# A channel mixer's first products in seven block products for eight, in a two-layer hybrid trunk

## The chip, the cores and the metric

One core of a Trainium2 chip runs the whole program. The metric is the device time of one execution in microseconds (us). TensorE multiplies matrices; VectorE (DVE in the rows), ScalarE (ACT) and GpSimd (POOL) work element by element; SyncE (SP) issues the loads. All data sits in an on-chip memory (SBUF); matmuls write into PSUM banks, which VectorE and ScalarE read.

## The reference

Two layers follow each other. Each has an attention part (three token mixers and projections), which the change leaves as it is, and then a channel mixer, cut here to what matters:

```python
def conv_glu(h, w1, conv_w, conv_b, w2):
    a, u = jnp.split(h @ w1, 2, axis=-1)
    a = dwconv_centred(a, conv_w) + conv_b
    return (jax.nn.silu(a) * u) @ w2
...
hl = modulate(xl, norm2_g[l], mod_l[3], mod_l[4])
xl = xl + mod_l[5] * conv_glu(hl, ffn_w1[l], ffn_conv_w[l], ffn_conv_b[l], ffn_w2[l])
```

`h` has 1024 features, `w1` maps them to 2 x 2816 columns, `w2` maps 2816 back to 1024. `modulate` is a root-mean-square norm with a scale and a shift per feature. The convolution runs over three neighbouring tokens. Layer 0 works on 512 latent and 256 context tokens (768), layer 1, the last, on the 512 latent ones alone.

## The kernel before, in words

Activations lie with features on the 128 partitions and tokens along the columns, so `h` is eight tiles of 128 features. Each float32 value is split into a rounded high half and a low half (the rest), and a product is three passes: high by high, low weight by high, high weight by low. A weight unit (`wunit`) loads up to 1024 columns as a raw tile (`wr`, two buffers), ACT writes the high half and VectorE or, for every third unit, GpSimd the low half into a tile `wl` (four buffers), and then the raw buffer is free. SP's queue holds the loads in program order, so a load that waits for a buffer holds back those behind it.

In the channel mixer (`mixer` in `layer`), w_1 is taken in 22 pairs of 128-column chunks, an a-chunk f and a u-chunk 22 + f. For each, 8 feature tiles x 3 passes = 24 matmuls of 512 columns, in layer 0 also 24 of 256, add up in a PSUM bank `pf`. `use_a` then makes the convolution and the first half of silu from the bank, `use_u` multiplies by u, `then` splits the result into `g`, high and low. After a group of five or six pairs (`FGROUPS`) `down` multiplies the group by w_2 into eight chunks of the result, each added to `x` by `residual`.

The order on each engine is fixed when the program is built: a planner (`sch`) holds jobs in program order, takes the matmuls of the current and the next one, and inserts the deferred work of other engines by estimated times. The norm ahead of the mixer (`norm_chain`) writes `hh` and `hl`; it starts when the sums of squares of the tokens are there, for layer 1 in two halves of 256 tokens, because there the last three chunks of w_o, the product before it, run in halves (`sg`).

Tile names in the rows: `wr`, `wl` weights raw and split; `x` the residual stream, `xn`, `hh`, `hl` the norm's results; `ff`, `g` the gated product; `th`, `acc` scratch; `pf`, `pm`, `pb` PSUM banks. All instructions go through one wrapper, so their line is L167 throughout; the raw loads have L500.

Of the kernel before, what the change touches and what calls it, by code (L numbers as in the profile page):

```python
# [34 lines left out]
FGROUPS = ((0, 6), (6, 6), (12, 5), (17, 5))  # L35
# [139 lines left out]
class Sched:  # L175
# [124 lines left out]

    def met(self, need):
        return need() if callable(need) else self.room(need)

    def piece(self):
# [35 lines left out]
        if self.cur is not None and self.nxt is None:  # L340
            n = len(self.jobs[0][1]) if self.jobs and self.jobs[0][0]() else 2
            if self.cur[0] + n + (self.parked[0][0] if self.parked else 0) <= NWL and (n <= 2 or self.left["w"] > NSLOT):
                self.nxt = self.pick()
# [35 lines left out]
def trunk(  # L379
# [19 lines left out]
    wl_ = ctx.enter_context(tc.tile_pool(name="wl", bufs=NWL))  # L399
# [93 lines left out]
    def wunit(src, n):  # L493

        while sch.left["r"] < 1:
            sch.flush([g for g in sch.groups if g[4]][:1])
        sch.left["r"] -= 1
        hl = wl_.tile([P, 2, 1024], F32R, tag="wl", name="wl")
        raw = wr_.tile([P, 1024], F32, tag="wr", name="wr")
        nc.sync.dma_start(out=raw[:, 0:n], in_=src)  # L500
        lo_n[0] += 1
        eng = "G" if lo_n[0] % lo_n[1] == 0 else "V"

        def halves():
# [1230 lines left out]
    for l in range(DEPTH):  # L1735
# [172 lines left out]
        hh, hl = h_tiles(nt)  # L1908
        ready = {"n": HALF if last else LAT}

        def fin(a, b, cond):
            sch.spawn(norm_chain(cond, stats, x, hh, hl, am, m48, 24, a, b, 0 if a < LAT else 1, ready), -1)
# [4 lines left out]
        sch.jobs.append((always, *fprojs(specs[-3:], mh, ml, nt, None, sg)))  # L1917
# [7 lines left out]

        def mixer():
            for f0, nf in FGROUPS:
                gh, gl_ = [], []
                for f in range(f0, f0 + nf):
                    ff = []  # L1930

                    def use_a(a, b, v, ps, f=f, ff=ff):
                        if not ff:
                            ff.extend(slot(2, nt, "ff"))
                        yield from conv(ff[0][:, a:b], ps, cf[:, f, :], bf[:, f:f + 1])
                        yield from silu2(ff[0][:, a:b], ff[1][:, a:b])
                        ff.append(a)

                    def use_u(a, b, v, ps, ff=ff):
                        yield lambda: a in ff[2:]  # L1940
                        yield "V"
                        V.tensor_tensor(out=ff[0][:, a:b], in0=ff[0][:, a:b], in1=ps, op=ALU.mult)

                    def then(ff=ff, gh=gh, gl_=gl_):
                        hi, lo = slot(2, nt, "g", F32R)
                        split(hi, lo, ff[0], G)
                        gh.append(hi)
                        gl_.append(lo)
                    specs = [(w_1[l, f], use_a, None), (w_1[l, FC + f], use_u, then)]
                    for e in [specs] if f == 0 else [specs[:1], specs[1:]]:  # L1950
                        yield fprojs(e, hh, hl, nt, KB, None, ready if f == 0 else None)
                end = f0 == FGROUPS[-1][0]

                def down(us, cs, gh=gh, gl_=gl_, nf=nf, end=end):
                    yield lambda: len(gl_) == nf
                    units = [(cols(u, 0), residual(x, gate2, c, post if end else None), None) for u, c in zip(us, cs)]
                    yield from mm3s(units, gh, gl_, nt, nf, None, True, sg if len(cs) > 1 else None)

                for cs in [(c,) for c in range(KC - 3)] + [(5, 6, 7)] if end else [(c,) for c in range(KC)]:
                    yield [(w_2[l, c, :, f0 * P:(f0 + nf) * P], nf * P) for c in cs], lambda us, cs=cs, down=down: down(us, cs)  # L1960
# [130 lines left out]
```

## Time and profile before

| | |
|---|---|
| median of 3 runs | 2910.19 us (2909.45 to 2910.57) |
| profiled execution | 2909.93 us |
| its span (first to last instruction) | 2908.2 us |
| granted TensorE clock, mean | 0.994 of full speed |
| TensorE busy | 2835.2 us, 97% |
| VectorE / ScalarE / GpSimd busy | 1699.2 / 1226.8 / 811.3 us |

The span is what the trace covers; the profiled time is 1.7 us longer. Busy shares are means over stages that differ: the mixer of layer 0 lies at about 1109 to 1662 us, that of layer 1 at about 2541 to 2905 us.

### The profile page before, as it was taken

Reading aid. Unit: us, or ns where it says so; the run is one execution under the profiler, and the core shown is the slowest. Engines: PE = TensorE matmul, PEld = TensorE weight load, DVE = VectorE, ACT = ScalarE, POOL = GpSimd, SP = SyncE. Lnnn points to the kernel's source line nnn. Section 1 sums busy time; section 2 is a strip of 40 time slices with the busy share of each in tenths; the row PEclk is TensorE's granted clock in tenths of the full one; section 3 lists DMA queues with packets and bytes.
Section 4 is the critical chain, followed back from the end, with each engine's and each line's share of the span. In section 5 each row is a group of like instructions: output and inputs, shape, how many; then the busy total and the mean of one; then the engine's idle time right before and its main releaser. Section 6 shows DMA issues by size and latency. Waiting matters only on the chain.

```text
span 2908.2 us, 48877 instructions
## 1 busy us (share of the span) xinstructions
PE 2835.2 (97%) x19304; PEld 2460.5 (85%) x19304; DVE 1699.2 (58%) x3433; ACT 1226.8 (42%) x2522; POOL 811.3 (28%) x832
## 2 busy tenths in 40 slices
PE   7999999999999999999999999999999999999999
PEld 5888898888788888888888889898878788888888
DVE  4555767868766545333334456577787866553343
ACT  4444556645443224222222345466654443343332
POOL 3414231123322432112112242441123333422221
PEclk9999999999999999999999999999999999999999
DMA  8242211241312631121212321212131316323332
GB/s 312 90 147 77 68 49 55 62 157 59 113 57 97 221 109 59 51 73 53 72 58 68 97 75 55 61 59 62 57 122 44 132 66 203 127 85 107 97 98 87
DMA packets 100117, 271.99 MB, mean 94 GB/s; under 512 B 14209, under 2 KB 26417, under 8 KB 99889
## 3 DMA queue, kind: packets, MB, share of 16 engines
q1 hardware_dynamic: 88800, 247.31, 26.5%
q10 hardware_dynamic: 10800, 20.98, 1.8%
q8 instruction: 152, 2.49, 0.4%
q0 software_dynamic: 288, 0.59, 0.1%
q14 instruction: 77, 0.62, 0.1%
HBM read 240.56 MB, written 28.86 MB: 93 GB/s over the span
## 4 chain that ended last, share of the span: by engine, by line
PE 56%; DVE 3%; POOL 2%; issue 1%; ACT 1%; DMA 1%; SPq 0%; POOLq 0%; ACTq 0%; DVEq 0%
PE pf L167 46%; PE pm L167 7%; PE pb L167 2%; DVE wl L167 0%; POOL wl L167 0%; POOL m L167 0%; POOL pres L167 0%; DVE mx L167 0%; DMA th<-gd 0%; DVE dnw L167 0%; DVE oacc L167 0%; DVE pres L167 0%; POOL rn L167 0%; POOL rtmp L167 0%; DVE p L167 0%
## 5 line engine op out<-in xcount | busy, mean ns | idle before, releaser
L167 PE MATMUL pf<-hh,wl 128*128 128x512 f32 (+1 forms) x4192 | 1022.6, 359 | 9.9 <-ACT hh L167 6.2
L167 PEld LDWEIGHTS pf<-hh,wl 128*128 128x128 f32 x4192 | 698.1, 190 | 105.0 <-ACT hh L167 9.2
L167 POOL TENSOR_TENSOR wl<-wr,wl 128x512 fp32r<-128x512 f32 (+3 forms) x258 | 326.0, 1280 | 940.0 <-ACT wl L167 934.1
L167 PE MATMUL pf<-hl,wl 128*128 128x512 f32 (+1 forms) x2096 | 575.7, 359 | 0.9 <-POOL hl L167 0.6
L167 ACT CAST wl<-wr 128x512 fp32r<-128x512 f32 (+3 forms) x620 | 341.2, 588 | 491.0 <-PE pf L167 423.4
L167 PEld LDWEIGHTS pf<-hl,wl 128*128 128x128 f32 x2096 | 361.0, 190 | 47.6 <-POOL hl L167 1.8
L167 PE MATMUL pf<-wl,hh 128*128 128x256 f32 (+2 forms) x1664 | 321.7, 288 | 0.0
L167 PE MATMUL pf<-g,wl 128*128 128x512 f32 (+1 forms) x1629 | 307.3, 350 | 0.0
L167 PEld LDWEIGHTS pf<-g,wl 128*128 128x128 f32 x1629 | 263.8, 189 | 42.3 <-ACT g L167 1.9
L167 DVE TENSOR_TENSOR wl<-wr,wl 128x512 fp32r<-128x512 f32 (+4 forms) x362 | 263.3, 751 | 51.5 <-ACT wl L167 49.7
L167 PEld LDWEIGHTS pf<-wl,hh 128*128 128x128 f32 x1664 | 264.5, 192 | 5.9 <-issue 4.1
L167 PE MATMUL pf<-wl,hl 128*128 128x256 f32 (+2 forms) x832 | 241.1, 290 | 0.0
L167 DVE SCALAR_TENSOR_TENSOR x<-pf,gate,x 128x512 f32<-128x512 f32 (+1 forms) x126 | 80.4, 640 | 243.6 <-PE pf L167 237.0
L167 PE MATMUL pm<-dnw,pres 128*128 128x128 f16 (+1 forms) x1824 | 195.3, 236 | 6.2 <-POOL pres L167 3.0
L167 DVE SCALAR_TENSOR_TENSOR ff<-pf,cf,ff 128x511 f32<-128x511 f32 (+1 forms) x132 | 86.9, 658 | 184.5 <-ACT ff L167 183.2
L167 ACT ACTIVATE p<-pb,nb,r 128x768 f32<-128x768 f32 (+1 forms) x160 | 145.1, 908 | 104.5 <-DVE nb L167 82.7
L167 PE MATMUL pf<-ohl,wl 128*128 128x512 f32 (+1 forms) x864 | 171.6, 359 | 1.5 <-DVE ohl L167 0.7
L167 PEld LDWEIGHTS pf<-ohl,wl 128*128 128x128 f32 x864 | 143.9, 191 | 26.4 <-DVE ohl L167 1.8
L167 PEld LDWEIGHTS pf<-wl,hl 128*128 128x128 f32 x832 | 160.1, 192 | 2.7 <-issue 2.5
L167 DVE TENSOR_REDUCE mx<-pb 128x1 f32<-128x768 f32 (+1 forms) x160 | 133.5, 845 | 41.1 <-PE pb L167 39.9
L167 ACT CAST dnw<-pm 128x512 f16<-128x512 f32 x144 | 83.9, 585 | 143.8 <-PE pm L167 140.3
L167 PEld LDWEIGHTS <-pres 128*128 128x128 f16 (+1 forms) x1440 | 87.3, 98 | 58.2 <-issue 32.3
(246 smaller groups left out, 4083.9 us busy)
## 6 DMA issues: line engine op xcount, KB each, us to landing
wm<-in_w_mod_dram SPq DMA_DIRECT2D x96, 512.0 KB, 5.4
wr<-in_w_dram SPq DMA_DIRECT2D x88, 512.0 KB, 3.6
wr<-in_w_f_dram SPq DMA_DIRECT2D x80, 512.0 KB, 3.6
wr<-in_w_t_dram SPq DMA_DIRECT2D x32, 512.0 KB, 3.7
wr<-in_w_br_dram SPq DMA_DIRECT2D x24, 512.0 KB, 3.6
wr<-in_w_dram SPq DMA_DIRECT2D x32, 384.0 KB, 3.1
wr<-in_w_dram SPq DMA_DIRECT2D x32, 320.0 KB, 2.9
gd<-th ACTq DMA_DIRECT2D x24, 384.0 KB, 2.3
```

What stands on the lines that cost most here:

```text
L167: ins = f(*args, **kw)
```

## The change

The first products of a pair of chunks are regarded as a 2 x 2 block product. The features are halved (four tiles of 128 each), the weights of a pair are the blocks a1, a2 (the a-chunk by upper and lower features) and u1, u2, and the tokens are halved too. With seven products of sums of blocks in place of eight products of blocks, the four result blocks come out as sums. Per pair that is 7 x 4 x 3 = 84 matmuls of half the tokens (384 columns in layer 0, 256 in layer 1), where there were 48 of 512 and, in layer 0, 48 of 256.

The sums have to be made. For the weights `block_weights` loads both raw tiles and holds them until four sums and seven splits into halves are done; for the activations `Blocks.fill` makes, after the norm, seven sets of four tiles (B11, B21, B22 and T1 to T4), split again. `block_products` runs the seven products into three banks and takes them out in seven evictions; `block_gated` makes convolution and gate from SBUF, with edges of one column where the halves of tokens meet. The tile `wl` of 2 x 1024 becomes two tiles of 1024, in all eight buffers. Groups are smaller in layer 0, one pair is run ahead of each group's w_2 products, and the w_2 units of layer 0 take two chunks each. w_o's last three chunks are no longer in halves in layer 1.

```diff
-FGROUPS = ((0, 6), (6, 6), (12, 5), (17, 5))
+FGROUPS = ((3, 3, 3, 3, 3, 3, 4), (6, 6, 5, 5))
...
-    wl_ = ctx.enter_context(tc.tile_pool(name="wl", bufs=NWL))
+    wl_ = ctx.enter_context(tc.tile_pool(name="wl", bufs=2 * NWL))
...
+            for k in range(KH):
+                plain("B22", k, KH + k, 1)
+
+                V.scalar_tensor_tensor(out=t(KH + k, 1), in0=t(KH + k, 1), scalar=self.dsh[:, k, v:v + 1], in1=t(k, 1), op0=ALU.add, op1=ALU.subtract)
+                G.tensor_tensor(out=t(k, 1), in0=t(k, 1), in1=t(k, 0), op=ALU.subtract)
+                V.scalar_tensor_tensor(out=t(k, 0), in0=t(KH + k, 1), scalar=sh(k), in1=t(k, 0), op0=ALU.add, op1=ALU.add)
+                summed("T2", k, k, 0, V)
+                yield 0
...
+    def block_weights(l, f, ops):
+
+        raws = []
+        for j in (f, FC + f):
+            yield lambda: sch.left["r"] > 0
+            sch.left["r"] -= 1
+            raw = wr_.tile([P, 1024], F32, tag="wr", name="wr")
+            nc.sync.dma_start(out=raw, in_=w_1[l, j])
+            raws.append(raw)
+        (a1, a2), (u1, u2) = [(r[:, 0:512], r[:, 512:1024]) for r in raws]
+
+        def operand(src, eng):
+            yield lambda: sch.ring() > 0
+            sch.held += 1
+            o = wl_.tile([P, 1024], F32R, tag="wl", name="wl")
+            yield "S"
+            S.copy(out=o[:, 0:512], in_=src)
+            yield eng
+            (G if eng == "G" else V).tensor_tensor(out=o[:, 512:1024], in0=src, in1=f32(o[:, 0:512]), op=ALU.subtract)
+            ops.append(o)
+
+        def add(out, p, q, op):
+            yield "G"
+            G.tensor_tensor(out=out, in0=p, in1=q, op=op)
+        yield from operand(a1, "V")
+        yield from operand(a2, "V")
+        yield from add(a1, a1, u1, ALU.subtract)
+        s2 = th_.tile([P, TOK], F32, tag="th", name="th")[:, 0:512]
+        yield from add(s2, u2, a1, ALU.subtract)
+        yield from operand(s2, "V")
+        yield from add(u1, u1, u2, ALU.add)
+        yield from operand(u1, "V")
+        yield from operand(a1, "G")
+        yield from add(a2, a2, s2, ALU.subtract)
+        yield from operand(a2, "V")
+        sch.left["r"] += 1
+        yield from operand(u2, "G")
+        sch.left["r"] += 1
...
+        for j, (nm, bk) in enumerate(zip(PROD, "ABADBDB")):
...
+            for i, (e, d) in enumerate(((0, 0), (1, 0), (0, 1))):
+                for k in range(KH):
...
+                    T.matmul(p, lhsT=ops[j][:, e * 512 + k * P:e * 512 + (k + 1) * P], rhs=bl.at(nm, k, d, c0, c1),
+                             start=(j < 5 and i == 0 and k == 0), stop=(i == 2 and k == KH - 1), skip_group_check=True)
...
+        yield "G"
+        G.tensor_tensor(out=y, in0=y, in1=u, op=ALU.mult)
+        yield "V"
+        V.scalar_tensor_tensor(out=y, in0=th, scalar=1.0, in1=y, op0=ALU.add, op1=ALU.mult)
+        yield "S"
+        S.copy(out=hi, in_=y)
+        yield "G"
+        G.tensor_tensor(out=lo, in0=y, in1=f32(hi), op=ALU.subtract)
...
-        sch.jobs.append((always, *fprojs(specs[-3:], mh, ml, nt, None, sg)))
+        sch.jobs.append((always, *fprojs(specs[-3:], mh, ml, nt)))
```

GpSimd's order in layer 1, inside a run of pairs. Before, its rows are low halves of every third weight unit and g's low half:

```order
722 L167 TENSOR_TENSOR wl<-wr,wl 128x512 [waits PE_49,DMAHW1_49,Activation_49,Pool_49]
723 L167 TENSOR_TENSOR wl<-wr,wl 128x512 [waits Activation_49]
724 L167 TENSOR_TENSOR g<-ff,g 128x512 [waits Activation_49]
725 L167 TENSOR_TENSOR wl<-wr,wl 128x512 [waits DMAHW4_49,Activation_49,Pool_49]
726 L167 TENSOR_TENSOR wl<-wr,wl 128x512 [waits Activation_49]
727 L167 TENSOR_TENSOR g<-ff,g 128x512 [waits Activation_49] x2
```

These rows span three pairs or so. Of the change, one pair (`wr<-wr` and `th<-wr` are sums of weights, `th<-th,au` is y times u):

```order
861 L167 TENSOR_TENSOR wr<-wr 128x512 [waits DMAHW1_49,DMAHW2_49,DVE_49,Pool_49]
862 L167 TENSOR_TENSOR th<-wr 128x512 [waits Pool_49]
863 L167 TENSOR_TENSOR wr<-wr 128x512
864 L167 TENSOR_TENSOR wr<-wr,th 128x512 [waits DVE_49,Pool_49]
865 L167 TENSOR_TENSOR wl<-wr,wl 128x512 [waits Activation_49]
866 L167 TENSOR_TENSOR wl<-wr,wl 128x512 [waits PE_49,Activation_49]
867 L167 TENSOR_TENSOR th<-th,au 128x512 [waits Activation_49]
868 L167 TENSOR_TENSOR g<-th,g 128x512 [waits Activation_49]
```

Eight instructions stand for one pair, the first of which waits for both loads, and the low halves come after all four sums; in other pairs y times u stands between the two low halves.

SP's order at the w_1 loads of layer 1, first before, where each load waits for one engine, GpSimd for every third:

```order
611 L500 DMA wr<-in_w_dram 128x1024 [waits DMAHW7_49,Pool_49]
612 L500 DMA wr<-in_w_dram 128x1024 [waits DMAHW0_49,DVE_49]
613 L500 DMA wr<-in_w_dram 128x1024 [waits DMAHW1_49,DVE_49]
614 L500 DMA wr<-in_w_dram 128x1024 [waits DMAHW2_49,Pool_49]
615 L500 DMA wr<-in_w_dram 128x1024 [waits DMAHW3_49,DVE_49]
```

And of the change, three pairs:

```order
622 L1842 DMA wr<-in_w_dram 128x1024 [waits DMAHW1_49,DVE_49,Pool_49]
623 L1842 DMA wr<-in_w_dram 128x1024 [waits DMAHW2_49,Pool_49]
624 L1842 DMA wr<-in_w_dram 128x1024 [waits DMAHW3_49,DVE_49,Pool_49]
625 L1842 DMA wr<-in_w_dram 128x1024 [waits DMAHW4_49,Pool_49]
626 L1842 DMA wr<-in_w_dram 128x1024 [waits DMAHW6_49,DVE_49,Pool_49]
627 L1842 DMA wr<-in_w_dram 128x1024 [waits DMAHW5_49,DVE_49]
```

Each pair's loads now wait for VectorE and GpSimd work on the pair before, in the two buffers.

VectorE's order in layer 1 at the norm before the mixer. Before, scalings (`xn<-pm,am,x`) and low halves (`hl`) of the first 256 tokens alternate, with weights and residuals between:

```order
2889 L167 SCALAR_TENSOR_TENSOR xn<-pm,am,x 128x256
2890 L167 SCALAR_TENSOR_TENSOR hl<-xn,modF,hh 128x256 [waits Activation_49]
2891 L167 SCALAR_TENSOR_TENSOR xn<-pm,am,x 128x256 x3
2892 L167 TENSOR_TENSOR wl<-wr,wl 128x512 [waits DMAHW0_49,PE_49]
2893 L167 SCALAR_TENSOR_TENSOR hl<-xn,modF,hh 128x256 [waits Activation_49]
```

Of the change, a part of the longer row of sums that follows the scalings (`xn<-xn` are sums, `bt` the home of T1, T2 and T4):

```order
3129 L167 SCALAR_TENSOR_TENSOR xn<-xn,dsh 128x256 [waits DVE_49] x2
3130 L167 SCALAR_TENSOR_TENSOR hh<-xn,modF,hh 128x256 [waits Activation_49]
3131 L167 SCALAR_TENSOR_TENSOR xn<-xn,modF 128x256 [waits Pool_49] x2
3132 L167 SCALAR_TENSOR_TENSOR xn<-xn,dsh 128x256 [waits DVE_49]
3133 L167 TENSOR_TENSOR bt<-xn,bt 128x256 [waits Activation_49]
```

The sums of one tile pass from VectorE to GpSimd and back before the block's halves can be made.

## Rows read from the trace of the kernel before

**Rows 1.** The page's head and busy time by engine

```profile
span 2908.2 us, 48877 instructions
...
PE 2835.2 (97%) x19304; PEld 2460.5 (85%) x19304; DVE 1699.2 (58%) x3433; ACT 1226.8 (42%) x2522; POOL 811.3 (28%) x832
```

**Rows 2.** The chain that ended last (start us, us, what)

```profile
1128.12 533.81 PE pf L167 x3065
...
2547.11 357.76 PE pf L167 x1646
```

**Rows 3.** Windows in both mixers (us, busy by engine, clock, DMA share, GB/s)

```profile
1200.00:1275.00 75.00, 75.00 (x433) 66.27 (x432) 25.34 (x43) 15.93 (x30) 10.75 (x9) 1.00 0.24 69
...
2700.00:2775.00 75.00, 75.00 (x331) 61.86 (x330) 30.14 (x46) 24.28 (x44) 15.53 (x14) 1.00 0.33 100
```

**Rows 4.** TensorE's timeline (start us, us, engine, line, operation, count)

```profile
1820.78 0.40 PE L167 MATMUL pf<-wl,hh 128*128 128x256 f32 x2
...
1827.62 0.40 PE L167 MATMUL pf<-wl,hh 128*128 128x256 f32 x2
...
2555.72 0.62 PE L167 MATMUL pf<-hl,wl 128*128 128x512 f32 x2
...
2574.77 0.62 PE L167 MATMUL pf<-hl,wl 128*128 128x512 f32 x2
```

**Rows 5.** A raw load in the chain, and DMA issues (size, us to landing)

```profile
1106.22 4.01 DMA wr<-in_w_dram
...
1110.31 0.62 ACT wl L167
...
wm<-in_w_mod_dram SPq DMA_DIRECT2D x96, 512.0 KB, 5.4
wr<-in_w_dram SPq DMA_DIRECT2D x88, 512.0 KB, 3.6
```

**Rows 6.** GpSimd's and VectorE's timelines where they meet

```profile
1166.10 1.84 POOL L167 TENSOR_TENSOR g<-ff,g 128x768 fp32r<-128x768 f32 x1 [13.08 <-ACT g L167]
1166.57 1.92 DVE L167 TENSOR_TENSOR wl<-wr,wl 128x512 fp32r<-128x512 f32 x1 [0.56 <-ACT wl L167]
...
2502.87 2.55 POOL L167 TENSOR_TENSOR wl<-wr,wl 128x512 fp32r<-128x512 f32 x2 [4.16 <-ACT wl L167]
2503.53 0.75 DVE L167 SCALAR_TENSOR_TENSOR x<-pf,gate,x 128x512 f32<-128x512 f32 x1 [0.61 <-PE pf L167]
...
2567.50 1.29 DVE L167 TENSOR_TENSOR wl<-wr,wl 128x512 fp32r<-128x512 f32 x2
```

**Rows 7.** GpSimd's groups by shape in layer 0's mixer (busy, mean ns)

```profile
L167 POOL TENSOR_TENSOR g<-ff,g 128x768 fp32r<-128x768 f32 x22 | 40.6, 1844 | 156.0 <-ACT g L167 156.0
...
L167 POOL TENSOR_TENSOR hl<-xn,hh 128x256 fp32r<-128x256 f32 x4 | 3.0, 740 | 9.5 <-ACT xn L167 9.5
```

**Rows 8.** Timelines at layer 0's norm: VectorE, then TensorE behind pair 0

```profile
1098.05 0.75 DVE L167 SCALAR_TENSOR_TENSOR x<-pf,gate,x 128x512 f32<-128x512 f32 x1 [4.69 <-PE pf L167]
...
1103.95 0.75 DVE L167 SCALAR_TENSOR_TENSOR xn<-pm,am,x 128x512 f32<-128x512 f32 x1 [0.76 <-PE pm L167]
...
1107.98 2.05 DVE L167 SCALAR_TENSOR_TENSOR xn<-pm,am,x 128x512 f32<-128x512 f32 x3
...
1123.98 0.87 DVE L167 SCALAR_TENSOR_TENSOR hl<-xn,modF,hh 128x256 fp32r<-128x256 f32 x2
...
1131.10 1.09 PE L167 MATMUL pf<-hh,wl 128*128 128x512 f32 x4
```

**Rows 9.** TensorE's timeline at layer 1's norm

```profile
2531.93 6.48 PE L167 MATMUL pf<-mhl,wl 128*128 128x256 f32 x52
2541.47 0.71 PE L167 MATMUL pf<-hh,wl 128*128 128x256 f32 x4 [3.06 <-DVE x L167]
...
2554.79 1.09 PE L167 MATMUL pf<-hh,wl 128*128 128x512 f32 x4
```

**Rows 10.** Windows with the granted clock (the column after POOL)

```profile
1731.00:1737.00 6.00, 5.54 (x30) 5.55 (x31) 0.98 (x1) 2.16 (x4) 0.70 (x1) 0.50 0.32 87
...
2538.40:2541.50 3.10, 0.04 (x2) 0.06 (x1) 3.10 (x4) 0.21 (x2) 2.25 (x2) 1.00 0.14 40
```

More of the change, by code (lines that the diff above doesn't have):

```diff
@@ L299, in take_up, with ring @@
         return [len(units), body([u for u, _ in units]), must, [g for _, g in units]]
+    def ring(self):
+        return 2 * (NWL - sum(j[0] for j in (self.cur, self.nxt, self.parked and self.parked[0]) if j)) - self.held
     def met(self, need):
@@ L341, in piece @@
             n = len(self.jobs[0][1]) if self.jobs and self.jobs[0][0]() else 2
-            if self.cur[0] + n + (self.parked[0][0] if self.parked else 0) <= NWL and (n <= 2 or self.left["w"] > NSLOT):
+            if (2 * n <= self.ring() and (n <= 2 or self.left["w"] > NSLOT)
+                    and (n == 0 or not self.held or self.left["r"] > 0 or any(g[4] for g in self.groups))):
                 self.nxt = self.pick()
@@ L497, in wunit @@
         sch.left["r"] -= 1
-        hl = wl_.tile([P, 2, 1024], F32R, tag="wl", name="wl")
+        hl = [wl_.tile([P, 1024], F32R, tag="wl", name="wl") for _ in range(2)]
         raw = wr_.tile([P, 1024], F32, tag="wr", name="wr")
-        nc.sync.dma_start(out=raw[:, 0:n], in_=src)
+        srcs = src if isinstance(src, list) else [src]
+        w = n // len(srcs)
+        for i, s in enumerate(srcs):
+            nc.sync.dma_start(out=raw[:, i * w:(i + 1) * w], in_=s)
         lo_n[0] += 1
@@ L1720, in trunk, with block_view @@
+    def block_view(t, H, a, b):
+        if H == LAT // 2:
+            return t[:, a:b]
+        c0, c1 = (0, LAT // 2) if a == 0 else (LAT // 2, H)
+        return t.rearrange("p (h c) -> p h c", h=2)[:, :, c0:c1]
     x = chunks8(TOK, "x")
@@ L1907, in trunk @@
         am = norm_gain(l, 1, m48)
[L1908 to L1909 removed]
+        bl = Blocks(nt)
         def fin(a, b, cond):
[L1912 removed]
+            sch.spawn(bl.chain(cond, stats, x, am, m48, a, b, 0 if a < LAT else 1), -1)
         add, stats = norm_acc(x, nt, None, fin, th_.tile([P, TOK], F32, tag="th", name="th"))
@@ L1924, in trunk @@
         V.tensor_scalar(out=gate2, in0=m48[:, 40:48, :], scalar1=0.5, scalar2=None, op0=ALU.mult)
-        def mixer():
[L1927 to L1960, printed above, removed]
@@ new lines, in trunk, with pair, body, run @@
+        gs = []
+        def pair(f):
+            def body(us):
+                ops, au = [], []
+                sch.defer(block_weights(l, f, ops))
+                def run():
+                    au.extend(slot(2, nt, "au"))
+                    if f == 0:
+                        cuts = [(0, LAT // 2)] + ([(LAT // 2, bl.H)] if bl.H > LAT // 2 else [])
+                    else:
+                        cuts = [(0, bl.H)]
+                    for c0, c1 in cuts:
+                        yield from block_products(bl, ops, au, c0, c1, f == 0, c1 == bl.H)
+                    sch.defer(block_gated(bl, au, cf, bf, f, gs))
+                return run()
+            return [], body
@@ new lines, in down, with body @@
+        def down(f0, nf, cs, end):
+            packed = len(cs) > 1 and not end
+            srcs = [w_2[l, c, :, f0 * P:(f0 + nf) * P] for c in cs]
+            def body(us):
+                yield lambda: len(gs) >= f0 + nf
+                uses = [residual(x, gate2, c, post if end else None) for c in cs]
+                order = [(s, i) for s in sg or segs(nt) for i in range(len(cs))] if len(cs) > 1 and end else [(s, i) for i in range(len(cs)) for s in segs(nt)]
+                for (a, b, v), i in order:
+                    ps = bank()
+                    w = cols(us[0], i * nf * P) if packed else cols(us[i], 0)
+                    for n, (e, d) in enumerate(((0, 0), (1, 0), (0, 1))):
+                        for k in range(nf):
+                            T.matmul(ps[:, 0:b - a], lhsT=w(k)[e], rhs=block_view(gs[f0 + k][d], bl.H, a, b),
+                                     start=(n == 0 and k == 0), stop=(n == 2 and k == nf - 1))
+                            yield
+                    sch.defer(uses[i](a, b, v, ps[:, 0:b - a]), ps)
+            return [(srcs, len(cs) * nf * P)] if packed else [(s, nf * P) for s in srcs], body
@@ new lines, in mixer @@
+        def mixer():
+            ahead, f0 = 0, 0
+            for nf in FGROUPS[l]:
+                end = f0 + nf == FC
+                while ahead < min(FC, f0 + nf + 1):
+                    yield pair(ahead)
+                    ahead += 1
+                if end:
+                    css = [(c,) for c in range(KC - 3)] + [(5, 6, 7)]
+                else:
+                    n = 2 if 2 * nf * P <= 1024 else 1
+                    css = [tuple(range(c, c + n)) for c in range(0, KC, n)]
+                for cs in css:
+                    yield down(f0, nf, cs, end)
+                f0 += nf
```

146 lines of the change are left out of this document (140 added, 6 removed).

## The prediction

> **What bounds the kernel now.** I read the page's head first: TensorE is busy for 97% of a span of 2908.2 us, VectorE for 58%, GpSimd for 28% [rows 1]. Then the chain of work that ended last: both channel mixers lie on it as one unbroken piece each, nothing but the matmuls into `pf`, 533.8 us in layer 0 and 357.8 us in layer 1 [rows 2]. The windows inside the mixers say the same: 75.00 us of TensorE in 75 us, GpSimd at 11 to 16 us and VectorE near 30 [rows 3]. So a matmul taken out of a mixer is worth its full pace, as long as the other engines keep up. The question is whether they still do, because the change pays for the saved products with additions on GpSimd and VectorE and with two raw weight buffers that are held longer.
>
> The profiled execution took 2909.93 us, 1.7 us more than its span and 0.26 us under the median of 2910.19. All sums are made against it; the forecast in median terms is 0.3 us higher, which is nothing here.
>
> **The change, part by part.**
>
> *Saved matmul time.* At a steady place 84 matmuls of 512 columns start within 2555.72 and 2574.77, 226.8 ns each; 57 of 256 columns start within 1820.78 and 1827.62, 120.0 ns each [rows 4]. No 384-column one is in the trace; scaling the one pace gives 170, the other 180, and the middle, (226.8 + 120.0)/2 = 173.4 ns, I take. Layer 0, per pair of chunks: before 48 x (226.8 + 120.0) = 16.65 us, after 7 x 12 = 84 x 173.4 = 14.57 us, 2.08 saved. Layer 1: before 48 x 226.8 = 10.89, after 84 x 120.0 = 10.08, 0.81 saved. For 21 pairs in each layer (pair 0 is counted below): 43.7 + 17.0 = **60.7 us saved**, between 49 and 67 by the two ends of the 384-column price. The Trainium skill (TensorE: Matmul & The Clock Gate, Back-to-back issue gap) gives N/2.4 + 2.5 ns for a matmul of N columns. As an estimate from that page, 2.0 and 1.2 us would be saved per pair, 66 in all; the rows' own paces lie 11 ns above it at either size, and I keep the rows.
>
> *GpSimd and VectorE do not run beside each other on data in SBUF.* At 1166.10 GpSimd starts a subtraction of 1.84 us; VectorE starts its own at 1166.57 and needs 1.92 us, ending 0.55 us after GpSimd's, where two such in a row take 1.29 us, 0.65 each. But a VectorE instruction with one operand in PSUM takes 0.75 us in the middle of two GpSimd ones [rows 6]. So a VectorE instruction with two SBUF operands waits until GpSimd's has ended. The Trainium skill says so in kind (GPSIMD Engine Reference, Specifications: the SBUF interfaces are shared with VectorE, with contention where a VectorE instruction has two SBUF inputs), without a price; the trace agrees, and shows the price to be the rest of the running GpSimd instruction.
>
> *Layer 1, a steady pair.* New on GpSimd are four 512-column sums and two low halves, beside y·u and g's low half: eight instructions of 1.28 us (2.55 for two [rows 6]), 10.2 us. VectorE has five low halves of weights, two convolution taps and the tanh gate with two SBUF operands: 8 x 0.65 = 5.2 us. Since the two exclude each other, 15.4 us of work stand against 10.08 us of TensorE. The evictions have an operand in PSUM and are not in this sum. The order inside a pair gives the same figure. From both raw tiles in: ACT's high half of a1 0.62 [rows 5], low halves of a1 and a2 2 x 0.65 (1.9); three sums 3.84 (5.8); s2's low half (6.4), the fourth sum (7.7), u1+u2's low half (8.4), GpSimd's low half of a1-u1 (9.6), a2-s2's low half (10.3), GpSimd's of u2 (11.5). Only now is the second of the only two raw buffers free; the next load took 4.01 us to be readable [rows 5]: 15.5. y·u, the gate and the convolution fit into that load's time. I take **15.5 us per pair**. Without the exclusion it is 1.3 + 6 x 1.28 + 4.0 = 13.0; with y·u ahead of the last low half and loads of 5.4 us, as for the modulation weights [rows 5], 18.2. All are over 10.08.
>
> TensorE doesn't wait that long for each pair, since each run of pairs starts with one prepared. Runs are 6 (after pair 0), 6, 5 and 4 pairs, with the w_2 products between. At a run's start the seventh operand's tile has just come free: high half, low half and load put the second pair's raw tiles at 0.62 + 1.28 + 4.0 = 5.9; its last product ends 11.5 + 1.44 later, at 18.8, each further pair 15.5 later. So the wait of a run of n is 18.8 + 15.5 (n-2) - 10.08 n = 5.42 n - 12.2: 20.3, 20.3, 14.9, 9.5: **65 us lost**. With 13.0 it is 2.92 n - 9.7, 22 us; with 18.2, 105.
>
> *Layer 0, a steady pair*: tiles of 768 take 1.84 us on GpSimd [rows 7], so 6 x 1.28 + 2 x 1.84 = 11.4, and 5 x 0.65 + 3 x 0.98 = 6.2 on VectorE: 17.6 against 14.57. But a run is three pairs, and 8 x 9 x (226.8 + 120.0) ns = 25.0 us of w_2 products follow: 3 x 17.6 and some 6 of w_2's low halves is 59 in 68.7. By the formula above 18.8 + 0.6 + 17.6 < 43.7. I cost it at 0; its cover is thin (rival 3).
>
> *Layer 0, the norm before pair 0.* It now makes seven sets of sums. The first 512 tokens are eight scalings of 512 from PSUM (2.05/3 = 0.68), 32 instructions of 256 on VectorE with two SBUF operands (0.87/2 = 0.435) [rows 8] and 12 of 256 on GpSimd (0.74 [rows 7]): 5.5 + 13.9 on VectorE, 13.9 + 8.9 exclusive. From VectorE's start at 1103.95 that is 19.4 to 28.3 us, and I take 25: 1129. The context's 256 tokens need the same instructions at half the width, 14 to 20 us more: 1147, and the last product. Pair 0 ended at 1131.10 [rows 8]; with 1149, **18 lost** (5 if GpSimd hinders nothing, 24 at most).
>
> *Layer 1, the norm.* w_o's last three chunks are no longer in halves: 72 x 226.8 ns for 144 x 120.0, so w_o ends 1 us sooner, at 2537.5 for 2538.4 [rows 9]. But the norm that began while the second halves ran now follows the end. From the last residual to the first scaling it took 1098.05 to 1103.95, 5.9 us [rows 8]: 2543.4, then 25 us as above and a last product of 1.4: 2570, against 2554.79 for the end of pair 0 [rows 9]: **16 lost** (10 to 19). TensorE idles for some 7 us there. A gap of 3.06 us left the clock at 1.00 [rows 9, 10]; it was 0.50, the 1.2 GHz level, at 1731 to 1737 [rows 10]. A fall here costs little, because TensorE waits anyway.
>
> *The last group.* Before, only a product, a high and a low half followed the last u-product: 0.65 + 0.62 + 1.28 = 2.6 us in layer 1. Now it is an eviction, a bias, two taps, a tanh, y·u, the gate, and the halves: 0.4 + 3 x 0.62 + 3 x 0.65 + 2 x 1.28 = 6.8; in layer 0 3.9 and 9.9. In the other groups one pair ahead covers it, in the last none does: 4.1 + 6.0 = **10 lost**.
>
> *At nothing*: one-column taps at the edges, VectorE's evictions (VectorE has the time), the additional issues on SP. The weight tile now comes in two halves, which reorders the attention stages a little; nothing is added there: 0, by my estimate up to 10 either way.
>
> Sum: -60.7 + 65 + 18 + 16 + 10 = +48 us, **2958 us**.
>
> **The rivals.** (1) *The weights keep up better*: the exclusion hinders the order little, 13.0 us per pair and 22 lost, and the norms cost 10 and 10: -60.7 + 22 + 20 + 10 = -9, 2901. For it: the excluded instructions may fall into the load's 4 us; against it: GpSimd alone needs 10.2 us a pair, over TensorE's 10.08, and still the load. It decides from a loop of about 13.5 down. (2) *Half of the exclusion is hidden*: a loop of 14.3 costs about 43 us, and with norms as forecast the sum is +26, 2936. (3) *Evictions queue too*: VectorE runs in order, and a low half that waits 1.3 to 1.8 us for GpSimd holds back an eviction, while a PSUM bank is wanted again after one product of 2.08 us. One us per pair in layer 0 is 21: 2979; with y·u ahead of the last low half in a third of the pairs, 2990 and more. (4) *No change*: terms between (1) and (2) cancel, around 2910.
>
> **How the numbers follow.** Forecast 0.50 (2942 to 2975), (1) 0.20, (2) 0.10, (3) 0.13, (4) 0.07. A measurement of this kernel tells 0.2%, 5.8 us, from none. Faster: most of (1), 0.18; same: the rest of (1) and most of (4), 0.08; slower: all else, 0.74. The range leaves out some 0.08 under 2898 and 0.1 over 2988.
>
> **What would show it.** In layer 1's runs TensorE idle 4 to 6 us per pair with ACT's or GpSimd's halves as what ends the wait; the loads 15 to 16 us apart; GpSimd near 70% busy there; VectorE's low halves at 1.3 us or more; layer 0's mixer full except pair 0. Wrong it would be if the pairs of layer 1 follow at 10 to 11 us, or if layer 0's runs show gaps too.

## The result and the profile after

The changed kernel takes 3097.4 us (median of 4 runs, 3091.18 to 3099.7), the one before 2909.82 (4 runs, 2907.74 to 2910.57): 1.064 times as long, 95% interval 1.0624 to 1.0661. The forecast had slower as the likeliest, but +48 us and at most 2988; it is +187.6. The head of the page, busy time by engine, and the granted clock in tenths for 40 slices (the profiled run took 3099.7 us):

```profile
span 3097.9 us, 51389 instructions
...
PE 2859.9 (92%) x19796; PEld 2535.8 (82%) x19796; DVE 2030.4 (66%) x3955; ACT 1328.7 (43%) x2696; POOL 1205.1 (39%) x1111
...
PEclk9999999999999989999999999999999999798999
```

TensorE's busy time rose by 24.7 us against [rows 1], although 60 us of matmul time were to be saved, and its idle time from 73 to 238 us. GpSimd gained 394 us of work, VectorE 331. Where the time went is read from TensorE's timeline: the start of the last attention product (`mhl`), of pair 0, of its end, and of layer 1's.

```profile
1053.56 1.55 PE L167 MATMUL pf<-mhl,wl 128*128 128x512 f32 x6
...
1124.74 2.12 PE L167 MATMUL pf<-hh,wl 128*128 128x256 f32 x13
...
1177.33 2.99 PE L167 MATMUL pf<-hh,wl 128*128 128x384 f32 x16
...
1739.54 1.63 PE L167 MATMUL pf<-hh,wl 128*128 128x512 f32 x5 [0.97 <-ACT hh L167]
...
2573.10 1.63 PE L167 MATMUL pf<-mhl,wl 128*128 128x512 f32 x6 [0.41 <-DVE th L167]
...
2659.62 3.04 PE L167 MATMUL pf<-hh,wl 128*128 128x256 f32 x24
```

The same marks of before stand at 1037.95, 1109.14, 1131.10, 1668.37, 2489.97 and 2554.79. Their differences give stages in us, and beside them the forecast's terms, sorted by stage:

| | attention 0 | w_o 0 | pair 0, layer 0 | rest of layer 0 | attention 1 | w_o and pair 0, layer 1 | rest of layer 1 |
|---|---|---|---|---|---|---|---|
| before | 1038.0 | 71.2 | 22.0 | 537.3 | 821.6 | 64.8 | 353.4 |
| after | 1053.6 | 71.2 | 52.6 | 562.2 | 833.6 | 86.5 | 438.3 |
| measured | +15.6 | 0 | +30.6 | +24.9 | +12.0 | +21.7 | +84.9 |
| forecast | 0 | 0 | +18 | -37.7 | 0 | +16 | +52 |

Every stage but w_o is off in the same direction; the largest miss is the rest of layer 0, 62.6 us. The windows of layer 0's pair 0 and of the two rests (us, busy by engine, clock, DMA share, GB/s), against full TensorE at clock 1.00 in [rows 3]:

```profile
1124.70:1177.30 52.60, 31.70 (x182) 29.07 (x181) 41.05 (x96) 23.77 (x65) 25.08 (x32) 0.68 0.06 20
1177.30:1739.50 562.20, 513.99 (x2848) 482.89 (x2847) 347.17 (x592) 189.47 (x314) 289.21 (x196) 0.97 0.22 67
2659.60:3097.00 437.40, 366.48 (x2339) 338.77 (x2337) 290.07 (x414) 155.80 (x291) 255.99 (x187) 0.93 0.26 80
```

By the forecast's own paces (173.4, 226.8 and 120.0 ns) TensorE's work is 489 us in the rest of layer 0 (21 x 14.57 + 528 x 0.347) and 331 in that of layer 1 (21 x 10.08 + 528 x 0.227). So TensorE is busy for 25 and 35 us longer than that, and the rest is waiting, 48 and 71 us. (Before, its busy time in the same stretches lies 4.5 and 1.7 us over such a sum.)

Part of the longer busy time is the clock. Mean clocks of 0.97 and 0.93 come about because TensorE's granted clock, at 1.00 for the most part, falls 7 and 14 times to 0.50, its 1.2 GHz level, for 30.7 and 58.0 us in all; each time TensorE waits just then or has just waited, 1.8 us in the shortest case. It is busy for 28.9 and 55.2 us at that level. With 12 matmuls at either level in the rows below (3.87 us for 2.24, and 2.93 for 1.60) I estimate that this costs some 12 and 25 us. What makes up the rest is open.

What ended the waits (us, times, longest), first for 1177.3 to 1739.5, then for 2690 to the end, last for pair 0:

```profile
PE pf L167 <- DVE au L167: 36.3, 15, 3.5
PE pf L167 <- ACT g L167: 5.7, 1, 5.7
PE pf L167 <- DVE x L167: 4.6, 6, 1.1
...
PE pf L167 <- ACT au L167: 33.5, 11, 4.7
PE pf L167 <- DVE au L167: 22.1, 18, 3.9
PE pf L167 <- DVE wl L167: 4.9, 6, 0.9
...
PE pf L167 <- ACT bt L167: 15.3, 5, 6.2
PE pm L167 <- DVE acc L167: 3.2, 1, 3.2
```

TensorE hardly ever waits for a weight half (`wl`, 4.9 us in layer 1). It waits for `au`, an eviction: a product's result has to leave its bank before the next may have it. One such wait in layer 0, on all engines:

```profile
1427.02 0.33 SPq L1842 DMA_DIRECT2D wr<-in_w_dram  x1
...
1430.85 1.35 POOL L167 TENSOR_TENSOR wr<-wr 128x512 f32<-128x512 f32 x1 [3.85 <-DMA wr<-in_w_dram]
...
1431.04 4.32 PE L167 MATMUL pf<-bt,wl 128*128 128x384 f32 x24
...
1434.77 1.75 POOL L167 TENSOR_TENSOR wr<-wr,th 128x512 f32<-128x512 f32 x1
...
1435.20 2.24 PE L167 MATMUL pf<-hh,wl 128*128 128x384 f32 x12
...
1436.49 1.81 POOL L167 TENSOR_TENSOR th<-th,au 128x768 f32<-128x768 f32 x1
...
1438.33 0.96 DVE L167 SCALAR_TENSOR_TENSOR th<-au,th 128x768 f32<-128x768 f32 x1 [2.96 <-POOL th L167]
...
1439.21 0.55 DVE L167 TENSOR_TENSOR au<-pf,au 128x384 f32<-128x384 f32 x1
...
1440.28 1.21 DVE L167 TENSOR_TENSOR au<-pf,au 128x384 f32<-128x384 f32 x2
...
1440.88 3.87 PE L167 MATMUL pf<-hh,wl 128*128 128x384 f32 x12 [3.44 <-DVE au L167]
```

A load issued at 1427.02 is readable at 1430.8; four sums on GpSimd follow; y times u, which is due already, stands behind them and runs at 1436.49; VectorE's gate waits for it 2.96 us; and the eviction that the product ahead wants stands behind the gate on VectorE, with one more eviction and a low half between. TensorE stops for 3.44 us. In layer 1 the same holds on ScalarE, whose copies take out the first product:

```profile
2772.05 1.29 POOL L167 TENSOR_TENSOR wr<-wr 128x512 f32<-128x512 f32 x1 [4.04 <-DMA wr<-in_w_dram]
...
2786.64 1.29 POOL L167 TENSOR_TENSOR wr<-wr 128x512 f32<-128x512 f32 x1 [3.99 <-DVE au L167]
...
2793.12 2.93 PE L167 MATMUL pf<-hh,wl 128*128 128x256 f32 x12 [3.92 <-DVE au L167]
...
2807.93 1.60 PE L167 MATMUL pf<-bt,wl 128*128 128x256 f32 x12
...
2826.83 1.14 ACT L167 CAST wl<-wr 128x512 fp32r<-128x512 f32 x2 [0.61 <-POOL wr L167]
2827.88 0.36 ACT L167 COPY au<-pf 128x256 f32<-128x256 f32 x1
...
2837.64 3.00 POOL L167 TENSOR_TENSOR wr<-wr 128x512 f32<-128x512 f32 x2 [0.68 <-DVE wl L167]
```

The copy at 2827.88 comes behind two high halves that waited for GpSimd's sums; TensorE goes on at 2828.3. After the wait at 2793.12, 12 matmuls take 2.93 us, at a granted clock of 0.50 (2793 to 2796), the 1.2 GHz level; the 12 at 2807.93 take 1.60 for the same work, at 1.00.

### The profile page after: what moved, and what is told of

It reads as the page before. It is cut to its first block, busy times and chain, and to the rows that moved or that the text cites. A ratio compares the mean times of both kernels' runs of the same rounds, so it can differ in the third digit from the quotient of the medians.

```text
span 3097.9 us, 51389 instructions
## 1 busy us (share of the span) xinstructions
PE 2859.9 (92%) x19796; PEld 2535.8 (82%) x19796; DVE 2030.4 (66%) x3955; ACT 1328.7 (43%) x2696; POOL 1205.1 (39%) x1111
## 5 line engine op out<-in xcount | busy, mean ns | idle before, releaser
L167 PE MATMUL pf<-hh,wl 128*128 128x256 f32 (+2 forms) x4208 | 892.0, 343 | 75.8 <-DVE au L167 62.0
L167 POOL TENSOR_TENSOR wl<-wr,wl 128x512 fp32r<-128x512 f32 (+4 forms) x288 | 377.2, 1322 | 704.8 <-ACT wl L167 544.1
L167 ACT CAST wl<-wr 128x512 fp32r<-128x512 f32 (+4 forms) x708 | 397.3, 592 | 467.1 <-PE pf L167 324.3
L167 DVE TENSOR_TENSOR wl<-wr,wl 128x512 fp32r<-128x512 f32 (+4 forms) x420 | 340.2, 829 | 113.1 <-ACT wl L167 88.9
L167 PE MATMUL pf<-bt,wl 128*128 128x256 f32 (+2 forms) x1620 | 284.2, 333 | 66.1 <-ACT au L167 34.0
L167 PEld LDWEIGHTS pf<-bt,wl 128*128 128x128 f32 x1620 | 268.6, 215 | 72.7 <-ACT au L167 36.8
L167 PE MATMUL pf<-hl,wl 128*128 128x512 f32 (+1 forms) x1024 | 287.8, 367 | 0.1
L167 PE MATMUL pm<-dnw,pres 128*128 128x128 f16 (+1 forms) x1824 | 202.0, 237 | 11.4 <-POOL pres L167 5.8
L167 PEld LDWEIGHTS pf<-hl,wl 128*128 128x128 f32 x1024 | 172.4, 190 | 20.2 <-DVE hl L167 1.7
L167 DVE SCALAR_TENSOR_TENSOR th<-au,cf,th 128x1 f32<-128x1 f32 (+2 forms) x264 | 148.3, 610 | 42.6 <-ACT th L167 42.4
L167 DVE TENSOR_TENSOR au<-pf,au 128x256 f32<-128x256 f32 (+2 forms) x270 | 128.9, 478 | 72.0 <-PE pf L167 66.6
L167 PEld LDWEIGHTS pf<-ohl,wl 128*128 128x128 f32 x864 | 142.9, 191 | 30.7 <-issue 2.8
```

The lines of the kernel that those rows point to most:

```text
L167: ins = f(*args, **kw)
```

## The experiments

Stages in us, from each kernel's profiled run and cut at the same marks (both attention stages summed; w_o 0 is 71.2 in each). The last column is the time of the profiled run, in the last three rows the median of 5, 10 and 10 runs:

| | attention | pair 0, layer 0 | rest 0 | w_o and pair 0, layer 1 | rest 1 | time |
|---|---|---|---|---|---|---|
| before | 1859.6 | 22.0 | 537.3 | 64.8 | 353.4 | 2909.93 |
| after | 1887.1 | 52.6 | 562.2 | 86.5 | 438.3 | 3099.7 |
| e_alias | 1859.6 | 52.4 | 560.1 | 84.7 | 434.9 | 3064.68 |
| e_delay | 1877.9 | 52.6 | 556.6 | 84.1 | 432.7 | 3076.77 |
| e_raw3 | 1926.8 | 55.5 | 541.0 | 84.3 | 417.1 | 3097.67 |
| e_yu_v | 1877.6 | 58.0 | 534.4 | 84.6 | 426.9 | 3054.45 |
| e_all_v | 1881.6 | 50.8 | 523.7 | 84.2 | 403.2 | 3016.65 |
| e_nosum | 1877.6 | 60.6 | 507.4 | 83.6 | 371.6 | 2973.80 |
| e_l0 | 1862.5 | 52.0 | 565.2 | 62.7 | 352.6 | 2968.04 |
| e_l0v | 1858.9 | 51.2 | 524.2 | 62.8 | 352.6 | 2922.9 |
| e_l0v_plain | 1859.9 | 54.7 | 522.8 | 64.3 | 352.6 | 2928.29 |
| e_late2 | 1860.3 | 33.2 | 535.3 | 62.8 | 352.6 | 2917.65 |
| e_late3 | 1856.2 | 33.3 | 530.6 | 62.8 | 352.6 | 2912.61 |

**The attention stages, which the change leaves as they are.** e_split puts the two-tile weights alone into the kernel before; e_alias lets the planner's clock take the two tiles of the changed kernel for one again.

```diff
-        hl = wl_.tile([P, 2, 1024], F32R, tag="wl", name="wl")
+        hl = [wl_.tile([P, 1024], F32R, tag="wl", name="wl") for _ in range(2)]
```

> The kernel before with one edit of the change alone: the split weight tile of 2 x 1024 becomes two tiles of 1024 from eight buffers. Both mixers keep their eight products. Theory A (the planner orders the attention stages differently because of the two tiles, and that alone costs the 28 us by which they grew): about 2937 us, TensorE's first product of w_o in layer 0 at 1054 instead of 1038 us, both mixers as long as before (559 and 367 us). Rival (the attention stages grew through the other edits, the packing of the residual tiles or the changed rule for taking up the next job): within 5 us of the kernel before.

```diff
-        name = ap.tensor.name
+        name = self.alias.get(ap.tensor.name, ap.tensor.name)
...
+        est.alias[hl[1].tensor.name] = hl[0].tensor.name
```

> The changed kernel with one edit in the planner's books: the two halves of a weight tile count as one piece of data again, as they did when they were one tile; every tile, buffer and instruction stays. If the attention stages grew because the planner's estimates saw two tiles (theory A): they come back to about 1038 and 822 us (from 1054 and 834), the mixers stay within 8 us, about 3070 us in all. If it is the buffers themselves: 1050 or more and 830 or more, about 3097.

e_split: 2929.52, 15.7 us over the kernel before on the same chip; its attention stages take 1051.0 and 828.0, 13.0 and 6.4 longer than before, its mixer of layer 0 560.0 for 559.3. e_alias brings the attention back to 1859.6 in sum (1047.0 and 812.6, so by stage it is another order still), and the kernel to 3064.68. So the 27.6 us there are the planner's: with two tiles its estimates change, and with them the order of deferred work.

**The source of the waits: sums, y times u, the load, the order.** All on the changed kernel.

e_yu_v, y times u from GpSimd to VectorE:

```diff
-        yield "G"
-        G.tensor_tensor(out=y, in0=y, in1=u, op=ALU.mult)
+        yield "V"
+        V.tensor_tensor(out=y, in0=y, in1=u, op=ALU.mult)
```

> The changed kernel with y times u on VectorE instead of GpSimd. Theory Q (TensorE's waits come from evictions that stand in VectorE's queue behind the gate, which waits for y times u, which stands in GpSimd's queue behind the next pair's sums): the 36 us of waits for VectorE in layer 0 mostly go, the stretch from the end of pair 0 to the mixer's end falls from 562 to about 530 us, and in layer 1 from 438 to about 420. Theory W (the pace of the weights' work on the two excluding engines, as forecast): 0.6 us per pair less in layer 1, about 425, and layer 0 unchanged at 562.

e_raw3, a third raw buffer (for one slot of another pool, which costs the attention 40 us, so that only its mixers are to be read):

```diff
-NSLOT = 15
+NSLOT = 14
...
-    wr_ = ctx.enter_context(tc.tile_pool(name="wr", bufs=2))
+    wr_ = ctx.enter_context(tc.tile_pool(name="wr", bufs=3))
```

> The changed kernel with three raw weight buffers instead of two (paid for with one working slot less, which reorders the attention stages, so only the mixers are read). If the loads that start late are the source of all the waits (the sums come late, and with them y times u, the gate and the evictions behind it): from pair 0 to the mixer's end layer 0 falls from 562 to about 525 us and layer 1 from 438 to about 395. If the work of GpSimd and VectorE that exclude each other is the limit by itself (15.4 us per pair): layer 1 stays above 425 and layer 0 gains under 10.

e_nosum, the four weight sums left out:

```diff
-            yield "G"
-            G.tensor_tensor(out=out, in0=p, in1=q, op=op)
+            return
+            yield
...
-        s2 = th_.tile([P, TOK], F32, tag="th", name="th")[:, 0:512]
+        s2 = u2
```

> The changed kernel with the four sums of weights per pair left out (the seven products run on plain blocks, so the result isn't the trunk's; loads, halves, products and evictions stay). Theories Q and W both: the waits go, layer 0 from pair 0 to the end 490 to 500 us instead of 562 (21 x 14.57 + 7 x 25.0 and the last group's wait), layer 1 340 to 350 instead of 438. If the waits come from the halves, the evictions or the tokens' edges instead: over 540 and over 410.

e_delay, the planner books the sums only once the loads are to be there:

```diff
+        t0 = est.t["P"]
+        yield lambda: est.t["P"] >= t0 + ROW_LOAD
```

> The changed kernel with the planner told that a pair's raw weights are there 3.5 us after their loads are issued (it books loads at no time), so that sums and halves take later places on every engine; work and TensorE's order stay. If evictions stand behind late work because the planner thought it early (theory Q in the form of a wrong order): from pair 0 to the mixer's end layer 0 falls from 562 to 535 us or less and layer 1 from 438 to 415 or less. If the weights' own pace decides (theory W): both within 8 us of 562 and 438, or longer.

e_all_v, e_yu_v and the sums on VectorE as well:

```diff
-            yield "G"
-            G.tensor_tensor(out=out, in0=p, in1=q, op=op)
+            yield "V"
+            V.tensor_tensor(out=out, in0=p, in1=q, op=op)
```

> The changed kernel with y times u and the four sums per pair on VectorE, so GpSimd keeps three low halves. Theory W (excluding work): 3 x 1.28 + 13 x 0.65 = 12.3 us per pair instead of 15.4, layer 1 from pair 0's end falls from 438 to about 390 us. Theory Q (evictions behind an instruction that waits for GpSimd): layer 0 falls from 562 to about 515, since no VectorE instruction waits for a chain of GpSimd's any more. Rival: VectorE becomes the bound itself in layer 1 (13 x 0.65 and seven evictions of 0.4 are 11.3 us of a pair's 10.08), with layer 1 over 420.

Against the changed kernel, rest 0 and rest 1 fall by 54.8 and 66.7 without the sums, by 38.5 and 35.1 with sums and y times u on VectorE, by 27.8 and 11.4 with y times u alone there, by 21.2 and 21.2 with a third raw buffer, by 5.6 and 5.6 with later booking. So the four sums are the main source in both layers, and a load that can start earlier takes away about a third. The 5.6 of the booking is no more than the changed kernel's own runs differ by (8.5 us).

Not all of the forecasts held. e_yu_v tells the theories apart in layer 0: 534.4 is near Q's 530, far from W's 562; in layer 1 426.9 lies nearer W's 425. e_raw3 comes out between its two. e_nosum falls short of both its figures by 7 and 22 us. e_delay is within W's 8 us. e_all_v, at 523.7 and 403.2, stays over Q's and W's numbers and under the rival's 420.

Without sums layer 0's clock is 0.99 and its rest 18 us over its 489; in layer 1 some waits stay even then (2600 to the end), their sum first, then one of them:

```profile
PE pf L167 <- DVE au L167: 20.9, 18, 1.6
...
2732.80 0.68 DVE L167 SCALAR_TENSOR_TENSOR th<-au,th 128x512 f32<-128x512 f32 x1
2733.39 0.68 DVE L167 TENSOR_TENSOR wl<-wr,wl 128x512 fp32r<-128x512 f32 x1
2734.00 0.94 DVE L167 TENSOR_TENSOR au<-pf,au 128x256 f32<-128x256 f32 x2
2734.47 1.70 PE L167 MATMUL pf<-hh,wl 128*128 128x256 f32 x12 [1.40 <-DVE au L167]
```

The evictions still stand behind the gate and a low half there. e_all_v is the one that shows a remedy: VectorE does a two-operand instruction of 512 in 0.65 us where GpSimd takes 1.28 [rows 6], and the due y times u is no longer kept on GpSimd behind a chain that began with a late load. The move is worth 74 us in the two rests, work and chain together. The Trainium skill (GPSIMD Engine Reference, When to use GPSIMD) puts elementwise work with two inputs on VectorE, GpSimd being about twice as slow; this trace agrees, with the 0.65 and 1.28 us.

**Is it the work, or the waiting in queues?** e_dummy gives the kernel before four more GpSimd sums per pair on data that nothing else wants, so GpSimd is as loaded as after, with no chain through the weights.

```diff
+                        for _ in range(4):
+                            G.tensor_tensor(out=ff[1][:, 0:512], in0=ff[1][:, 0:512], in1=ff[0][:, 0:512], op=ALU.add)
```

> The kernel before with four more GpSimd additions of 512 columns per pair of chunks, on scratch that nothing reads; result and all else stay. They are the GpSimd work of the change's four sums without the chain that they stand in (raw load, sums, halves, return of the buffer). If the sums hurt by the time in which GpSimd and VectorE exclude each other: the mixers grow by 20 us or more (layer 1's pairs then have some 10.5 us of excluding work in 10.89). If they hurt only by the chain, and by what stands behind it in the queues: the whole stays within 6 us of the kernel before.

2919.92 for 2909.14, +10.8, of which 5.6 in the mixer of layer 0 and 3.8 in that of layer 1: more than the 6 us that were to speak for the chain alone, less than the 20 that were to speak for the exclusion. The one wait of TensorE that is new is for GpSimd's `g` (1100 to 1680, then 2540 to the end); for VectorE it waits no longer than before:

```profile
PE pf L167 <- POOL g L167: 4.4, 4, 1.3
...
PE pf L167 <- POOL g L167: 2.8, 4, 0.8
```

The window of 2560 to 2900 (columns as above) shows the exclusion at work: for 136.62 us of VectorE in the kernel before it has 175.29, with three instructions fewer, and TensorE loses 2.80. First the kernel before, then e_dummy:

```profile
2560.00:2900.00 340.00, 340.00 (x1520) 281.29 (x1519) 136.62 (x212) 110.30 (x204) 79.60 (x68) 1.00 0.33 98
...
2560.00:2900.00 340.00, 337.20 (x1484) 277.07 (x1483) 175.29 (x209) 113.19 (x208) 209.37 (x158) 1.00 0.31 96
```

So at this load VectorE is stretched by GpSimd, and next to nothing waits for it. Four sums per pair on the way from the load to the halves are another thing: leaving them out of the changed kernel gains 122 us in the two rests. What exclusion alone costs where both engines' work together exceeds the pair's time was not tried.

**The change in layer 0 alone.** e_l0 takes layer 1 back to the old mixer (and has e_alias); e_l0v adds e_all_v's two edits.

```diff
-        sch.jobs.append((always, *fprojs(specs[-3:], mh, ml, nt)))
+        sch.jobs.append((always, *fprojs(specs[-3:], mh, ml, nt, None, sg)))
...
-        sch.jobs += [(always, *job) for job in mixer()]
+        sch.jobs += [(always, *job) for job in (mixer_old if last else mixer)()]
```

> The block products in layer 0 alone: layer 1 has its eight products, its norm in halves and its groups as before; the planner books a weight tile's halves as one. If the layers' losses add up: attention about 1038 and 822 us, layer 0's mixer 615 as in the changed kernel, layer 1's w_o and mixer 418 as before, about 2966 us in all. A time of 2955 or less or of 2980 or more would say that the layers or the stages act on each other.

> Block products in layer 0 alone, as in the run before with layer 1 as it was, and in addition the sums and y times u on VectorE. If the parts add up: layer 0 from pair 0's end 524 us (as with all sums on VectorE), pair 0 still 51, the rest as with layer 0 alone: about 2926 us. Rival: over 2945, if VectorE's gain in layer 0 came with an order that layer 1 had changed.

2968.04 and 2922.9, for 2966 and 2926: the parts add up. In e_l0v the rest of layer 0 is 13.1 us shorter than before, a gain at last, and pair 0 29.2 longer takes it away.

**Pair 0.** e_l0v_plain runs pair 0 in eight plain products, so that it needs no sums; e_l0v_plain2 two pairs. e_late2 and e_late3 (two and three plain pairs) also hold the activations' sums until pair 0 has run; e_late2p spreads them.

```diff
+        if plain:
+            yield from operand(a1, "V")
+            yield from operand(u1, "G")
+            yield from operand(a2, "V")
...
+            yield from operand(u2, "V")
...
+                        if f < NPLAIN:
+                            yield from plain_products(bl, ops, au, c0, c1, c1 == bl.H)
```

> As the run beside it, and pair 0 of layer 0 in eight plain products, so that the sums of activations are made while TensorE works on pair 0 (one block more, T4 made after pair 0). If pair 0's price is the time that the sums take with TensorE idle: pair 0 from 51 to about 25 us, some 3 us of waits in pair 1, total about 2902, faster than the kernel before by 0.2 to 0.4%. If the sums then stop pair 1 instead: pair 1's waits over 12 us, total 2910 to 2925.

> The same with pairs 0 and 1 of layer 0 in eight plain products. It gives up 2.1 us of saving and gives the sums 16 us more to be made. If pair 1 waits for the sums in the run beside it by more than 2 us, this one is faster by the difference; if not, it is 2 us slower, about 2904.

```diff
+            yield lambda: self.p0_done
...
-                yield 0
+                yield 700
```

> Block products in layer 0 alone with sums of weights and y times u on VectorE, pairs 0 and 1 plain, and now the sums of activations begin only after pair 0's products are issued. If the queue was pair 0's price (residuals and evictions behind the sums): pair 0 falls from 65 us (two plain pairs, sums at once: pairs 0 and 1 together) to 22 + 17 = 39, and the sums have pair 1's 17 us to be made in, of the 25 that they take; total about 2902. If the latency is what counts: TensorE waits the missing 8 us and more in pair 2, total 2912 to 2928.

> The same with pairs 0, 1 and 2 plain: 33 us of cover for sums that take 25, at 2.1 us of saving given up. If cover is what was lacking: no waits at the norm any more, pairs 0 to 2 in 22 + 2 x 16.7 = 55 us, total about 2898. If not faster than the run beside it by 2 us or more, the waits aren't for cover.

> As the run with two plain pairs, and the steps of the sums are booked 0.7 us apart, so that evictions and weights stand between them on VectorE. Queue: faster than without the gaps, below 2902. Latency: slower, since the sums are ready later.

e_l0v_plain missed: 2928.29, 1.0068 times before (1.0055 to 1.0080), its pair 0 at 54.7 us longer than e_l0v's, not shorter. TensorE's and VectorE's timelines show why:

```profile
1136.09 0.47 DVE L170 SCALAR_TENSOR_TENSOR x<-pf,gate,x 128x256 f32<-128x256 f32 x1
...
1136.61 1.65 PE L170 MATMUL pf<-bt,wl 128*128 128x256 f32 x6 [13.02 <-DVE x L170]
```

TensorE's next product waits 13.02 us, until w_o's last residual has emptied its PSUM bank, and on VectorE that stood behind 12 us of sums for later pairs: again an eviction in a queue. (The norm of the context's tokens needs this residual too and comes after it.) e_l0v_plain2 is the same, 2928.18, for the 2904 that were expected. With the sums held until pair 0 has run, pair 0 takes 33 us and e_late2 2917.65, 1.0026 (1.0016 to 1.0035): over the 2902 forecast for the queue and within the range for the latency, though its pair 0 is 21 us shorter than e_l0v_plain's. e_late3 gave 2912.61, 1.0008 (0.9999 to 1.0018), which can't be told from before; it is 5 us faster than e_late2, so cover was part of what was lacking, but it stays far from the 2898 forecast. e_late2p gave 2912.59 in one run, inside the spread of e_late2's ten, and settles nothing. No version here beats the kernel before.

What is left in e_late3's pair 0 (windows, as above, then TensorE's timeline):

```profile
1130.00:1140.00 10.00, 9.13 (x72) 8.34 (x71) 9.43 (x29) 6.63 (x20) 3.54 (x5) 1.00 0.13 50
1140.00:1150.00 10.00, 9.16 (x49) 9.02 (x49) 9.38 (x21) 4.59 (x15) 6.27 (x9) 0.61 0.00 0
```

```profile
1134.08 5.67 PE L170 MATMUL pf<-hh,wl 128*128 128x128 f32 x45 [0.22 <-ACT au L170]
...
1142.15 2.80 PE L170 MATMUL pf<-bt,wl 128*128 128x128 f32 x12 [0.84 <-DVE au L170]
1144.75 8.62 PE L170 MATMUL pf<-hh,wl 128*128 128x128 f32 x36
```

The context's 256 tokens are halved too, and in an unbroken stream at clock 1.00 matmuls of 128 columns start 112 ns apart (20 of them from 1134.74 to 1136.98), hardly less than the 120.0 of 256 columns [rows 4]. Then, behind a wait of 0.84 us for an eviction, the clock falls to its 1.2 GHz level (0.61 is the mean of the second window), and they start 213 ns apart, the 12 from 1142.15 on and 24 more. The last row's other 12 are pair 1's first, of 384 columns.

## Why the prediction was right in direction and wrong in size

*Saved matmul time* held where TensorE ran at clock 1.00: 24 matmuls of 384 columns start within 1431.04 and 1435.20, 173.3 ns each, for 173.4. Of the 60.7 us saved some 12 and 25 went again at the lower clock, by the estimate above. The sum has no term for the clock; of its one pause the prediction says "A fall here costs little, because TensorE waits anyway". That holds only while TensorE waits; the matmuls that follow the wait pay.

*"Layer 0, a steady pair ... I cost it at 0; its cover is thin (rival 3)"*, and under *At nothing*, "VectorE's evictions (VectorE has the time)": this is the step that failed, and the costliest miss, 62.6 us, of which 36.3 are waits for those evictions. The sum of the engines' work did fit in layer 0. The prediction's own sign of being wrong, "if layer 0's runs show gaps too", came true. What was left out is that the engines that empty the banks work in order, and that an eviction stands behind instructions that wait: the gate for y times u, y times u for sums, the sums for the load. Rival 3 named the queue but saw one low half of 1.3 to 1.8 us ahead of the eviction, 1 us per pair, 21 in all; the waits are up to 3.5 us, and the clock falls with them. The Trainium skill (TensorE: Matmul & The Clock Gate, Architectural detail) has ScalarE's, VectorE's and GpSimd's queues as strictly first in, first out; the 2.96 and 3.44 us above agree.

*Layer 1, a steady pair*: the loop of 15.5 us was near. GpSimd's first sums of five pairs start at 2772.05, 2786.64, and so on to 2837.64: 16.4 us each on average, 14.6 at the least. But the loop was taken as a wait for weights, with TensorE at full pace once they are there. The waits are for evictions (55.6 of 63.1 us), and some 25 us at the lower clock stand beside them, so the rest of layer 1 lost 84.9 and not 52. That the direction came out right is in part luck: the 65 us that decided it were to be waits for weight halves, and TensorE waited 4.9 us for those. *The exclusion* is seen, though weaker: VectorE's low halves here take 0.99 and 1.17 us on average (busy, mean ns, 2690 to 3060), where alone they take 0.65 [rows 6]:

```profile
L167 DVE TENSOR_TENSOR wl<-wr,wl 128x512 fp32r<-128x512 f32 x74 | 72.2, 985 | 29.2 <-ACT wl L167 27.8
L167 DVE TENSOR_TENSOR wl<-th,wl 128x512 fp32r<-128x512 f32 x19 | 22.2, 1170 | 24.7 <-ACT wl L167 24.5
```

*The norms*: 30.6 and 21.7 for 18 and 16 (2570 less 2554.79 is 15, so the second term is 1 us too high). The waits for T sums (`bt`, 15.3 us) were in the sum; the clock of 0.68 in layer 0's pair 0 and the 128-column matmuls of the context, which save next to nothing, were not. *The last group*: one wait of 5.7 us for `g` in layer 0, where 6.0 was forecast; right. *"The weight tile ... reorders the attention stages a little; nothing is added there: 0, by my estimate up to 10 either way"*: 27.6, shown by e_split and e_alias to be the planner's view of the tile. What stays open is the part of the exclusion in layer 1's 84.9 us, since e_all_v and e_nosum take away chain and exclusion together; e_yu_v, which parts the two in layer 0, does not do so in layer 1.

## What to carry to other kernels

Busy time that fits is no proof of cover: for every instruction that empties a PSUM bank, list what stands ahead of it in its engine's queue and what that waits for, back to the load. Matmul time saved by additions on other engines was lost twice here where they broke TensorE's stream, once as waiting and once as matmuls at the lower clock. And a tile cut in two, for whatever reason, is also a change to a planner's estimates; measure that alone first.

## What the runs showed of the hardware

In e_late3 TensorE's clock fell to its 1.2 GHz level behind a wait of 0.84 us, after a stretch of 10 us at 1.00 in which it was busy for 9.13. What set it off, no run tells. Matmuls of 128 columns started 112 ns apart at 1.00, where those of 256 start 120.0 apart, and 213 at the lower level. Four extra GpSimd instructions per pair beside VectorE's work cost 9.4 us in the mixers over 44 pairs, 0.2 us each pair, though they stretched VectorE's busy time from 136.62 to 175.29 us in 340.
